# Attention and decay masks: added by VectorE instead of by TensorE

## The chip, the cores and the metric

One core of a Trainium2 chip runs the whole program. The metric is the device time of one execution in microseconds (us), taken as the median of several runs. The engines are TensorE (PE, matrix products; PEld is its weight load), VectorE (DVE), ScalarE (ACT), GpSimd (POOL) and SyncE (SP, which issues the DMAs here).

## The reference

The reference is a decoder trunk of two layers over 256 tokens with a model width of 1024, in float32. Each layer is a feed-forward half step, a mixing step, a second feed-forward half step and an input embedding. The mixing step projects the normalised tokens once and feeds two mixers from it: a gated recurrent one in matrix form (four heads of 256, causal, with learned decay) and an attention with a window of 128 tokens (16 query heads of 64, 4 key heads, a learned sink for each head). Cut to what matters here:

```python
scores = einsum(q, k) * 64 ** -0.5
scores = where(valid, scores, -inf)            # a causal band of 128
mx = maximum(max(scores, -1), sink)
pr = exp(scores - mx)
den = sum(pr, -1) + exp(sink - mx)
out = einsum(pr / den, v)

dlog = where(causal, b_t - b_s + i_s, -inf)    # the recurrent mixer's decays
w_intra = exp(dlog - m_t)
s = einsum(q, k) * w_intra
```

## The kernel before

The kernel keeps its tokens as two tiles of 128 rows (`NT` = 2). Every product with a weight is made of three: weights and activations are split into a high part (`wh`, written by ScalarE) and a low part (`wl`, written by VectorE from the raw weight minus the high part), and TensorE adds up high x high, high x low and low x high in PSUM. A weight unit of 128x1024 is called a part; a ring of eight parts (`RING`) lies between the splitting and TensorE. Raw weights of 1 MB come in by DMA, two parts each.

The four engines' queues are written out by hand, in the order in which the program's Python code runs. A planner, `Clock`, keeps a modelled time for each engine: it charges each product its output columns at 2400 to the microsecond and each VectorE instruction 0.12 us and its columns at 960 to the microsecond (`COST`, line 65; `charge`, line 92). Work beside the main products runs in chains: Python generators that give out some instructions and then yield. `tick` (line 196) is called between products and advances each chain whose modelled inputs are ready. So what TensorE finds next in its queue is fixed before the run, by modelled times. TensorE takes its queue in that order, and so do VectorE and ScalarE.

A layer's jobs are, in order: the first feed-forward block (65 parts), then in the mixing step the projection to keys, values and queries (`kvq`, 12 parts), the recurrent values (`v`, 8), a gate (`gt`, 8), recurrent queries and keys (`z`, 8), the attention's output product (`ya`, 8), the output gate (`og`), `z`, `gt`, `ym`, `yo`, and after these the second feed-forward block and the embedding.

The attention's chains lie beside `kvq`, `v` and `gt`. `groups` (called from `mix`) starts one `scores` chain for each pair of key heads p and each token tile t, four a layer. `scores` handles two key heads (g = 0, 1), each with four query heads, and takes S = 128 keys at t = 0 (four heads to a PSUM bank, one round) and S = 256 keys at t = 1 (two heads to a bank, two rounds). Six such rounds, called blocks here, make up a layer. In a block TensorE first adds the mask into each bank with one product of 512 columns (the identity in bf16 times the band, `sc<-band,identb`), then adds the score products, which use 64 rows of the array each (`sc<-kT,qT`). VectorE takes the maxima of all heads of a bank in one reduction (`mx<-sc`) and combines them with the sinks (`mx<-mx,nsink`). ScalarE takes the exponentials from PSUM into an SBUF slot (`pr<-sc,mx`) with the row's sum as a second output. The `outputs` chain (line 1220) divides (`pr<-pr,dn`), transposes on TensorE (`tp<-ident,pr`), splits the result (`ptd`) and multiplies by the values (`ha`).

`decays` (line 1017), beside `z` and `ya`, makes for each of four recurrent heads a bank of 384 columns: one product that spreads the decay rows (`wt<-rows,pick`), two masks of 128 columns on TensorE (`wt<-mask_st,identb`), and three exponentials by ScalarE (`w<-wt,gcols`). The `head` chain uses them later: its products are `st`, and VectorE multiplies by the decays (`ws<-st,w`).

PSUM has eight banks, handed out in rotation to all of these.

Of the kernel before, what the change touches and what calls it, by code (L numbers as in the profile page):

```python
# [13 lines left out]
BF16 = mybir.dt.bfloat16  # L14
AF = mybir.ActivationFunctionType
ALU = mybir.AluOpType
AX = mybir.AxisListType
PSUM = bass.MemoryType.PSUM

P = 128  # L20
# [12 lines left out]
NEG = -1e30  # L33
# [130 lines left out]
class Trunk:  # L164
# [84 lines left out]
    def consts(self):  # L249
        nc, c = self.tc.nc, self.const  # L250
        self.ident = c.tile([P, P], F32, name="ident")
        make_identity(nc, self.ident)
        self.identb = c.tile([P, P], BF16, name="identb")
        nc.vector.tensor_copy(self.identb, self.ident)
        self.mhalf = c.tile([P, 32], F32, name="mhalf")
        nc.vector.memset(self.mhalf, -0.5)
        self.h = [c.tile([P, D], F32, name=f"h{t}") for t in range(NT)]
        self.ones = c.tile([MH, P], F32, name="ones")
        nc.vector.memset(self.ones, 1.0)
        self.pick = c.tile([P, MH], F32R, name="pick")  # L260
        self.rows2 = c.tile([P, T + P], F32R, name="rows2")
        for x in (self.pick, self.rows2):
            nc.gpsimd.memset(x.bitcast(F32), 0.0)
        for r in (slice(0, MH), slice(32, 32 + MH)):
            nc.vector.tensor_copy(self.pick[r], self.ident[r, r])

        def mask(out, base, step, channel):

            nc.gpsimd.memset(out, 0.0)
            nc.gpsimd.affine_select(out=out, in_=out, compare_op=ALU.is_ge, fill=NEG, base=base,  # L270
                                    pattern=[[step, P]], channel_multiplier=channel)

        self.mask_st = c.tile([P, P], BF16, name="mask_st")
        mask(self.mask_st, 0, 1, -1)
        self.band = c.tile([P, 2 * P], BF16, name="band")
        mask(self.band[:, :P], -1, 1, -1)
        mask(self.band[:, P:], 0, -1, 1)
# [607 lines left out]
class Mlstm:  # L885
# [131 lines left out]
    def decays(self):  # L1017

        tr, nc = self.tr, self.nc
        N = T + P  # L1020
        for hd in range(MH):
            ps = tr.bank("wt")[:, :N]
            nc.tensor.matmul(ps, tr.pick[:, hd : hd + 1].to_broadcast([P, P]), tr.rows2, start=True, stop=False,
                             skip_group_check=True)
            for o in (slice(0, P), slice(T, N)):
                nc.tensor.matmul(ps[:, o], tr.identb, tr.mask_st, start=False, stop=True, skip_group_check=True)
            yield
            if hd % 2 == 0:
                two = tr.slot("w")[:, : 2 * N].rearrange("p (h t) -> p h t", h=2)
            w = two[:, hd % 2, :]  # L1030
            for i in range(3):
                o = slice(i * P, (i + 1) * P)
                nc.scalar.activation(w[:, o], ps[:, o], AF.Exp, bias=self.cols[:, i, hd : hd + 1])
            self.w.append(w)
            yield
# [61 lines left out]
class Swa:  # L1097
# [85 lines left out]
    def scores(self, t, p, acc, chains):  # L1183


        tr, nc = self.tr, self.nc
        S = (t + 1) * P
        per = NB // S
        tok = slice(t * P, (t + 1) * P)
        rows = [slice(g * AD, (g + 1) * AD) for g in range(2)]  # L1190
        hd = [slice(4 * (2 * p + g), 4 * (2 * p + g) + 4) for g in range(2)]
        pr = [tr.slot("pr")[:, : 4 * S].rearrange("p (j s) -> p j s", j=4) for _ in range(2)]
        mx, den = ([tr.col(n, 4) for _ in range(2)] for n in ("mx", "dn"))
        mask = tr.band[:, None, 2 * P - S :].to_broadcast([P, per, S])
        for j0 in range(0, 4, per):
            js = slice(j0, j0 + per)
            ps = [tr.bank("sc").rearrange("p (j s) -> p j s", j=per) for _ in range(2)]
            for g in range(2):
                nc.tensor.matmul(ps[g], tr.identb, mask, start=True, stop=False, skip_group_check=True)
            for j in range(per):  # L1200
                for x, y in ((0, 0), (0, 1), (1, 0)):
                    for g in range(2):
                        nc.tensor.matmul(ps[g][:, j, :], self.qT[x](4 * p + j0 + j, tok, p=rows[g]),
                                         self.kT[rows[g], y, p, :S], start=False, stop=x == 1, skip_group_check=True)
            yield
            for g in range(2):
                nc.vector.tensor_reduce(mx[g][:, js], ps[g], axis=AX.X, op=ALU.max)
                nc.vector.scalar_tensor_tensor(mx[g][:, js], mx[g][:, js], -0.125, self.nsink[:, hd[g]][:, js],
                                               op0=ALU.mult, op1=ALU.min)
            yield  # L1210
            for g in range(2):
                for j in range(per):
                    i = j0 + j
                    nc.scalar.activation(pr[g][:, i, :], ps[g][:, j, :], AF.Exp, scale=0.125, bias=mx[g][:, i : i + 1],
                                         accum_out=den[g][:, i : i + 1])
        for g in range(2):
            chains.append(tr.later(self.outputs(t, p, g, acc, hd[g], pr[g], mx[g], den[g])))
            self.haT.written(chains[-1], 4 * p, 4, t)
# [63 lines left out]
```

## Time and profile before

| | |
|---|---|
| median of three runs | 1383.12 us (1381.99 to 1383.64) |
| profiled execution | 1383.27 us |
| its span, first to last instruction | 1381.5 us |
| TensorE busy | 1366.2 us (99%) |
| VectorE busy | 860.7 us (62%) |
| ScalarE busy | 734.8 us (53%) |
| mean granted TensorE clock | 0.998 |

The profile is that of one execution. Its busy times are sums of drawn durations. On TensorE products are pipelined and their ends are modelled, so successive ones overlap in the drawing, and the distance between two starts tells what a product takes of the queue. An engine that is not the bound can be idle at no cost. In the rows an idle time in brackets names what ended it.

### The profile page before, as it was taken

How to read it: one execution, taken by the hardware profiler on the slowest of the kernel's cores; microseconds unless marked ns; L12 is line 12 of the kernel's file. 1: busy time of each engine (PE TensorE's matmuls, PEld its weight loads, DVE VectorE, ACT ScalarE, POOL GpSimd, SP SyncE). 2: the span in 40 equal slices, each digit the busy share in tenths (PEclk: the TensorE clock that was granted, in tenths of full speed). 3: DMA queues.
4: the chain of work that ended last, by engine and by line, in shares of the span. 5: the costliest groups of instructions: out<-in, count | busy, mean ns of one | idle time of the engine just before them, and what ended most of it. 6: DMA issues, size and time to landing. Idle time of an engine off the chain costs nothing.

```text
span 1381.5 us, 21941 instructions
## 1 busy us (share of the span) xinstructions
PE 1366.2 (99%) x9056; PEld 1233.3 (89%) x9056; DVE 860.7 (62%) x1213; ACT 734.8 (53%) x1146; POOL 55.4 (4%) x84
## 2 busy tenths in 40 slices
PE   8999999999999999999999999999999999999998
PEld 5999887899899899988879998878998998999886
DVE  5655458767786665554565554687677876554544
ACT  5554346878465444443454443477785554544433
POOL 0000012000000000000000000120000000000000
PEclk9999999999999999999999999999999999999999
DMA  6665636344645565565456566445456544755651
GB/s 206 222 212 168 229 125 212 123 138 110 226 153 185 167 213 186 169 232 184 158 162 213 170 199 213 152 154 173 106 143 206 181 156 164 220 190 187 209 180 61
DMA packets 125830, 243.81 MB, mean 176 GB/s; under 512 B 14977, under 2 KB 23841, under 8 KB 125730
## 3 DMA queue, kind: packets, MB, share of 16 engines
q1 hardware_dynamic: 125730, 242.41, 55.1%
q8 instruction: 71, 1.16, 0.4%
q14 instruction: 29, 0.24, 0.1%
HBM read 241.34 MB, written 1.05 MB: 175 GB/s over the span
## 4 chain that ended last, share of the span: by engine, by line
PE 96%; DMA 1%; DVE 1%; ACT 1%; issue 0%; POOL 0%; SPq 0%; ACTq 0%; POOLq 0%
PE dn L130 17%; PE pg L130 16%; PE pu L130 14%; PE gu L130 7%; PE z L130 7%; PE gt L130 7%; PE kvq L130 5%; PE ya L130 3%; PE v L130 3%; PE ym L130 3%; PE yo L130 3%; PE og L130 3%; PE tp L130 3%; PE sc L130 1%; PE ha L130 1%; DMA raw<-in_ffn_w_gate_dram 1%
## 5 line engine op out<-in xcount | busy, mean ns | idle before, releaser
L130 DVE TENSOR_TENSOR wl<-raw,wh 128x1024 fp32r<-128x1024 f32 (+1 forms) x448 | 540.2, 1222 | 351.3 <-ACT wh L130 348.5
L130 ACT CAST wh<-raw 128x1024 fp32r<-128x1024 f32 x448 | 460.5, 1050 | 414.1 <-PE dn L130 82.9
L130 PE MATMUL dn<-wh,hid 128*128 128x512 f32 x688 | 218.1, 395 | 0.0
L130 PE MATMUL pg<-uT,wh 128*128 128x256 f32 x1088 | 194.0, 281 | 0.0
L130 PE MATMUL pu<-uT,wh 128*128 128x256 f32 x1088 | 192.9, 280 | 0.0
L130 PEld LDWEIGHTS pg<-uT,wh 128*128 128x128 f32 x1088 | 166.4, 188 | 0.2
L130 PEld LDWEIGHTS pu<-uT,wh 128*128 128x128 f32 x1088 | 166.2, 188 | 0.0
L130 PEld LDWEIGHTS dn<-wh,hid 128*128 128x128 f32 x688 | 129.2, 188 | 30.2
L130 PE MATMUL pg<-uT,wl 128*128 128x256 f32 x544 | 152.4, 280 | 0.0
L130 PE MATMUL pu<-uT,wl 128*128 128x256 f32 x544 | 152.2, 280 | 0.0
L130 PE MATMUL dn<-wl,hid 128*128 128x512 f32 x352 | 139.0, 395 | 0.0
L130 PEld LDWEIGHTS pu<-uT,wl 128*128 128x128 f32 x544 | 102.4, 188 | 0.0
L130 PEld LDWEIGHTS pg<-uT,wl 128*128 128x128 f32 x544 | 102.3, 188 | 0.0
L130 PE MATMUL z<-uT,wh 128*128 128x256 f32 x512 | 93.5, 284 | 0.0
L130 PE MATMUL gt<-uT,wh 128*128 128x256 f32 x512 | 93.1, 283 | 0.0
L130 PE MATMUL gu<-wh,uT 128*128 128x512 f32 x256 | 83.4, 402 | 2.2 <-ACT uT L130 2.2
L130 PEld LDWEIGHTS gt<-uT,wh 128*128 128x128 f32 x512 | 78.8, 188 | 1.2
L130 PEld LDWEIGHTS dn<-wl,hid 128*128 128x128 f32 x352 | 66.1, 188 | 15.1
L130 PEld LDWEIGHTS z<-uT,wh 128*128 128x128 f32 x512 | 78.8, 188 | 0.6
L130 PE MATMUL z<-uT,wl 128*128 128x256 f32 x256 | 71.9, 281 | 0.0
L130 PE MATMUL gt<-uT,wl 128*128 128x256 f32 x256 | 71.8, 280 | 0.0
L130 PE MATMUL kvq<-wh,uT 128*128 128x512 f32 x192 | 63.7, 401 | 0.0
(194 smaller groups left out, 2037.7 us busy)
## 6 DMA issues: line engine op xcount, KB each, us to landing
raw<-in_w_in_dram SPq DMA_DIRECT2D x60, 1024.0 KB, 5.1
raw<-in_ffn_w_up_dram SPq DMA_DIRECT2D x40, 1024.0 KB, 5.1
raw<-in_ffn_w_down_dram SPq DMA_DIRECT2D x40, 1024.0 KB, 5.2
raw<-in_ffn_w_gate_dram SPq DMA_DIRECT2D x39, 1024.0 KB, 5.5
raw<-in_w_branch_a_dram SPq DMA_DIRECT2D x16, 512.0 KB, 5.9
raw<-in_w_branch_m_dram SPq DMA_DIRECT2D x8, 1024.0 KB, 5.1
raw<-in_w_out_dram SPq DMA_DIRECT2D x8, 1024.0 KB, 5.2
raw<-in_ple_gate_w_dram SPq DMA_DIRECT2D x8, 1024.0 KB, 8.0
```

The costliest lines, as they stand in the source:

```text
L130: return issue(*args, **kw)
```

## The change

The bf16 copy of the identity goes. In `decays` the two mask products go; after the row product the chain yields, then VectorE adds the mask to the two blocks of 128 columns in place in PSUM, the chain yields again, and ScalarE takes the exponentials as before. In `scores` the mask product of each bank goes, and the first score product of a bank starts the bank. For each query head VectorE runs one instruction that adds the mask to the head's scores, writes the sum to the SBUF slot `pr` and gives the row's maximum as a second output; it takes the place of the one reduction over all heads of the bank. ScalarE then takes the exponentials from `pr` into `pr`.

```diff
@@ -250,8 +250,6 @@
         nc, c = self.tc.nc, self.const
         self.ident = c.tile([P, P], F32, name="ident")
         make_identity(nc, self.ident)
-        self.identb = c.tile([P, P], BF16, name="identb")
-        nc.vector.tensor_copy(self.identb, self.ident)
         self.mhalf = c.tile([P, 32], F32, name="mhalf")
         nc.vector.memset(self.mhalf, -0.5)
         self.h = [c.tile([P, D], F32, name=f"h{t}") for t in range(NT)]
@@ -1020,14 +1018,14 @@
         N = T + P
         for hd in range(MH):
             ps = tr.bank("wt")[:, :N]
-            nc.tensor.matmul(ps, tr.pick[:, hd : hd + 1].to_broadcast([P, P]), tr.rows2, start=True, stop=False,
-                             skip_group_check=True)
+            nc.tensor.matmul(ps, tr.pick[:, hd : hd + 1].to_broadcast([P, P]), tr.rows2, start=True, stop=True)
+            yield
             for o in (slice(0, P), slice(T, N)):
-                nc.tensor.matmul(ps[:, o], tr.identb, tr.mask_st, start=False, stop=True, skip_group_check=True)
-            yield
+                nc.vector.tensor_tensor(ps[:, o], ps[:, o], tr.mask_st, op=ALU.add)
             if hd % 2 == 0:
                 two = tr.slot("w")[:, : 2 * N].rearrange("p (h t) -> p h t", h=2)
             w = two[:, hd % 2, :]
+            yield
             for i in range(3):
                 o = slice(i * P, (i + 1) * P)
                 nc.scalar.activation(w[:, o], ps[:, o], AF.Exp, bias=self.cols[:, i, hd : hd + 1])
@@ -1191,27 +1189,29 @@
         hd = [slice(4 * (2 * p + g), 4 * (2 * p + g) + 4) for g in range(2)]
         pr = [tr.slot("pr")[:, : 4 * S].rearrange("p (j s) -> p j s", j=4) for _ in range(2)]
         mx, den = ([tr.col(n, 4) for _ in range(2)] for n in ("mx", "dn"))
-        mask = tr.band[:, None, 2 * P - S :].to_broadcast([P, per, S])
+        mask = tr.band[:, 2 * P - S :]
         for j0 in range(0, 4, per):
             js = slice(j0, j0 + per)
             ps = [tr.bank("sc").rearrange("p (j s) -> p j s", j=per) for _ in range(2)]
-            for g in range(2):
-                nc.tensor.matmul(ps[g], tr.identb, mask, start=True, stop=False, skip_group_check=True)
             for j in range(per):
                 for x, y in ((0, 0), (0, 1), (1, 0)):
                     for g in range(2):
                         nc.tensor.matmul(ps[g][:, j, :], self.qT[x](4 * p + j0 + j, tok, p=rows[g]),
-                                         self.kT[rows[g], y, p, :S], start=False, stop=x == 1, skip_group_check=True)
+                                         self.kT[rows[g], y, p, :S], start=j + x + y == 0, stop=x == 1,
+                                         skip_group_check=True)
             yield
             for g in range(2):
-                nc.vector.tensor_reduce(mx[g][:, js], ps[g], axis=AX.X, op=ALU.max)
+                for j in range(per):
+                    i = j0 + j
+                    nc.vector.tensor_tensor_reduce(pr[g][:, i, :], ps[g][:, j, :], mask, 1.0, NEG, op0=ALU.add,
+                                                   op1=ALU.max, accum_out=mx[g][:, i : i + 1])
                 nc.vector.scalar_tensor_tensor(mx[g][:, js], mx[g][:, js], -0.125, self.nsink[:, hd[g]][:, js],
                                                op0=ALU.mult, op1=ALU.min)
             yield
             for g in range(2):
                 for j in range(per):
                     i = j0 + j
-                    nc.scalar.activation(pr[g][:, i, :], ps[g][:, j, :], AF.Exp, scale=0.125, bias=mx[g][:, i : i + 1],
+                    nc.scalar.activation(pr[g][:, i, :], pr[g][:, i, :], AF.Exp, scale=0.125, bias=mx[g][:, i : i + 1],
                                          accum_out=den[g][:, i : i + 1])
         for g in range(2):
             chains.append(tr.later(self.outputs(t, p, g, acc, hd[g], pr[g], mx[g], den[g])))
```

## Rows read from the trace of the kernel before

**Rows 1.** The page: one line of part 1 (busy us, share of the span, count, by engine) and the first line of part 4 (shares of the chain that ended last).
```profile
PE 1366.2 (99%) x9056; PEld 1233.3 (89%) x9056; DVE 860.7 (62%) x1213; ACT 734.8 (53%) x1146; POOL 55.4 (4%) x84
...
PE 96%; DMA 1%; DVE 1%; ACT 1%; issue 0%; POOL 0%; SPq 0%; ACTq 0%; POOLq 0%
```

**Rows 2.** Busy time by stretch: stretch, its us, busy us and count of PE, PEld, DVE, ACT and POOL, granted clock, DMA share, GB/s. The attention of layer 0 and the end of layer 0.
```profile
238.00:268.00 30.00, 30.00 (x172) 23.81 (x169) 22.60 (x49) 25.90 (x74) 2.87 (x10) 1.00 0.36 108
268.00:301.00 33.00, 32.54 (x260) 30.26 (x259) 19.81 (x38) 26.33 (x71) 0.00 (x0) 1.00 0.41 137
...
656.00:700.00 44.00, 41.02 (x183) 33.26 (x182) 26.06 (x35) 22.68 (x39) 2.56 (x3) 0.96 0.41 131
```

**Rows 3.** The waits of TensorE over the whole span: who waited for whom, us in total, times, longest.
```profile
PE tp L130 <- DVE xn L130: 3.9, 2, 3.0
...
PE sc L130 <- DVE ptd L130: 0.9, 2, 0.5
```

**Rows 4.** The instructions on the tiles `sc` and `wt`: durations in ns (least, median, most), first and last start, forms with counts.
```profile
L130 PEld LDWEIGHTS sc<-kT,qT x192: 182/186/189, 234.5 to 970.5; 64*128 64x128 f32 x192
...
L130 PE MATMUL sc<-band,identb x24: 376/384/390, 233.9 to 969.7; 128*128 128x512 bf16 x24
...
L130 PE MATMUL wt<-mask_st,identb x16: 219/224/230, 322.8 to 1020.9; 128*128 128x128 bf16 x16
```

**Rows 5.** TensorE's products in order of time around the first score block: start, us drawn, engine, line, operation, tiles, count.
```profile
233.69 0.39 PE L130 MATMUL kvq<-wh,uT 128*128 128x512 f32 x1
233.92 0.61 PE L130 MATMUL sc<-band,identb 128*128 128x512 bf16 x2
234.46 1.56 PE L130 MATMUL sc<-kT,qT 64*128 64x128 f32 x24
```

**Rows 6.** The same around the last score block of layer 0.
```profile
284.96 0.39 PE L130 MATMUL sc<-band,identb 128*128 128x512 bf16 x1
285.82 0.38 PE L130 MATMUL sc<-band,identb 128*128 128x512 bf16 x1 [0.46 <-DVE ptd L130]
286.12 0.98 PE L130 MATMUL sc<-kT,qT 64*128 64x256 f32 x12
```

**Rows 7.** The same around the first decay head of layer 0.
```profile
322.64 0.34 PE L130 MATMUL wt<-rows,pick 128*128 128x384 f32 x1
322.82 0.29 PE L130 MATMUL wt<-mask_st,identb 128*128 128x128 bf16 x2
322.92 0.48 PE L130 MATMUL z<-uT,wh 128*128 128x256 f32 x2
```

**Rows 8.** Groups of instructions of the whole span by shape: count, busy us, mean ns of one, idle time before them.
```profile
L130 DVE TENSOR_TENSOR wl<-raw,wh 128x1024 fp32r<-128x1024 f32 x444 | 535.4, 1222 | 344.9 <-ACT wh L130 342.1 <-PE pg L130 1.9
...
L130 ACT ACTIVATE pr<-sc,mx 128x256 f32<-128x256 f32 x32 | 14.8, 492 | 0.0
...
L130 ACT ACTIVATE pr<-pr,dn 128x256 f32<-128x256 f32 x32 | 13.3, 505 | 0.0
...
L130 DVE TENSOR_REDUCE mx<-sc 128x2 f32<-128x512 f32 x16 | 11.0, 686 | 5.6 <-PE sc L130 5.4
...
L130 DVE SCALAR_TENSOR_TENSOR og<-num,rd,og 128x256 f32<-128x256 f32 x16 | 7.7, 484 | 0.6
...
L130 DVE TENSOR_TENSOR vpad<-kvq,vpad 128x128 fp32r<-128x128 f32 x8 | 2.3, 286 | 0.7 <-ACT vpad L130 0.7
...
L130 DVE TENSOR_TENSOR_SCAN gates<-ones,gates 4x128 f32<-4x128 f32 x6 | 2.3, 403 | 0.1
...
L130 DVE TENSOR_TENSOR sg<-sg,pu 128x256 f32<-128x256 f32 x4 | 1.7, 422 | 4.8 <-PE pu L130 4.8
```

**Rows 9.** VectorE in order of time behind the first score blocks.
```profile
237.57 0.17 DVE L130 SCALAR_TENSOR_TENSOR mx<-mx,nsink 128x4 f32<-128x4 f32 x1
...
239.51 0.16 DVE L130 SCALAR_TENSOR_TENSOR mx<-mx,nsink 128x2 f32<-128x2 f32 x1
```

**Rows 10.** VectorE's weight subtractions (tile `wl`) from the start of the span to two moments: stretch, its us, busy us and count, granted clock, DMA share, GB/s.
```profile
0.00:238.50 238.50, 100.01 (x84) 1.00 0.61 199
...
0.00:346.20 346.20, 130.41 (x109) 1.00 0.56 175
```

**Rows 11.** ScalarE in order of time behind the same blocks: the first exponential of the second group of the first block, and the first of the second block.
```profile
240.24 0.38 ACT L130 ACTIVATE pr<-sc,mx 128x128 f32<-128x128 f32 x1
...
241.61 0.52 ACT L130 ACTIVATE pr<-sc,mx 128x256 f32<-128x256 f32 x1
```

**Rows 12.** ScalarE's divisions of the first block, and TensorE's transposes of them, in order of time.
```profile
252.04 1.27 ACT L130 ACTIVATE pr<-pr,dn 128x128 f32<-128x128 f32 x4
...
253.87 0.60 PE L130 MATMUL tp<-ident,pr 128*128 128x128 f32 x4
```

**Rows 13.** VectorE and ScalarE in order of time beside the last decay head of layer 0.
```profile
332.52 5.79 DVE L130 SCALAR_TENSOR_TENSOR cv<-z,feat,cv 128x255 f32<-128x255 f32 x12 [0.23 <-ACT cv L130]
...
338.83 2.36 DVE L130 TENSOR_TENSOR wl<-raw,wh 128x1024 fp32r<-128x1024 f32 x2
...
337.88 0.90 ACT L130 ACTIVATE w<-wt,gcols 128x128 f32<-128x128 f32 x3
```

**Rows 14.** TensorE in order of time at the first recurrent head of layer 0.
```profile
348.86 1.49 PE L130 MATMUL st<-qk,qk 128*128 128x256 f32 x12
```

## The prediction

> **What bounds the kernel now.** I read the busy shares first. TensorE is busy 1366.2 us, 99% of the span, VectorE 62%, ScalarE 53%, and 96% of the chain of work that ended last is TensorE [rows 1]. So the time is the sum of what TensorE issues, and the other two engines matter only where they make it wait. The stretches say where that happens. In the attention part of layer 0, 238 to 301 us, TensorE is busy 62.5 of 63 us at the full granted clock (1.00, that is 2.4 GHz); 3 us are idle at the layer's end, 656 to 700 [rows 2]. In the list of TensorE's waits these have names: 3.9 us for normalised rows, which nothing here touches, and 0.9 us, in two waits, for a PSUM bank in the attention [rows 3]. What is taken from TensorE's queue in these stretches should therefore come off the time nearly whole, if the chains beside it still finish in time.
>
> **What is removed from TensorE.** The 24 mask products of the scores (384 ns each as drawn) and the 16 of the decays [rows 4]. Drawn durations overlap; what counts is the distance between starts. Before a score block, full-width products start every 0.23 us: the last at 233.69, the two masks from 233.92, and the first score product at 234.46 [rows 5]. The pair thus takes 0.54 us, of which 2 x 0.23 = 0.46 is the products and 0.08 the change to half-height tiles. Without the masks that change follows an ordinary product. If it then costs nothing the pair was worth 0.54; if the scores' weight load (0.186 us, [rows 4]) now stands open instead, 0.54 - 0.19 = 0.35. I take 0.46, since the change of tiles stays and masks and products have the same size. Twelve pairs (24 masks): 12 x 0.46 = 5.5 us, bounds 4.2 and 6.5.
>
> At one block in each layer the gain is smaller. At 284.96 the first mask starts, the second waits until 285.82 for a bank that VectorE frees (the subtraction for `ptd`), and the scores start at 286.12 [rows 6]. Without masks the scores wait for the same bank and can start at 285.82: 0.30 in place of 0.46, for two layers -0.3 us. The scores' own banks come free earlier than now (VectorE is their last reader, no longer ScalarE), but that is not the bank waited for here, so I count nothing for it.
>
> In the decays the row product starts at 322.64, the two masks at 322.82 and the next weight product at 322.92 [rows 7]: 0.10 us for a pair. Eight pairs: 0.8 us, or nothing if the next product's weight load, hidden behind the masks now, stands open. The cast copy of the identity at the start goes too; it lies under the first loads and is worth nothing.
>
> Sum on TensorE: 5.5 - 0.3 + 0.8 = 6.0 us.
>
> A page differs a little. The Trainium skill, "TensorE: Matmul & The Clock Gate", section "Wait — 56ns, not 53.3ns?", gives 2.4 GHz columns plus some 2.5 ns for each product, 215.7 ns at 512 columns and 55.6 ns at 128. By it the 40 masks were worth 24 x 0.2157 + 16 x 0.0556 = 6.1 us where the rows give 5.5 + 0.8 = 6.3 us; the rows' 0.23 us is the larger, and the sum keeps it.
>
> **What is added to VectorE.** A score block is two groups of four (128 keys) or two of two (256 keys) heads. Today each group is one reduction of 128x512, 686 ns [rows 8], and a small minimum, which stays. Then there are 32 sum-and-maximum instructions of 128x128 and 32 of 128x256, in place of 24 reductions. The trace has no such instruction. From below: a plain two-input operation, 286 ns at 128 columns and 422 at 256 [rows 8]. From above: the scan, which carries a value along the row as the maximum does, 403 ns at 128 columns [rows 8]; going by its excess over the plain one (0.117 us at 128, twice that at 256) some 656 at 256. I take the three-input operation, 484 ns at 256 [rows 8], and with the step of 136 ns between the plain ones some 350 at 128, because three operations on one element are nearest to it. VectorE's work: 32 x 0.35 + 32 x 0.484 = 26.7 us for 24 x 0.686 = 16.5; with the decay adds, 16 x 0.286 = 4.6, it grows by 14.8 us, 7.4 a layer. That is not on TensorE's path as long as two covers hold.
>
> First cover: the split weights. Behind the longer block on VectorE stand weight subtractions (1222 ns each, [rows 8]). By 238.5 us 84 of them have begun [rows 10]; the first feed-forward block uses 65 parts and the projection to queries, keys and values 12, so 7 are ahead when the values start there. A part lasts 12 products of 0.23 us, 2.8 us: a lead of some 19 us against some 1 us of delay a block. If this cover were gone, each block would cost its overrun, 0.6 to 1.4 us.
>
> Second cover: ScalarE's exponentials start late anyway. A block of 128-key heads grows from 1.37 to 8 x 0.35 = 2.8 us, so its last minimum, now at 237.57 to 237.74, moves to 239.2; the second group's first exponential is at 240.24, behind those of the first group [rows 9, 11]. Slack 2.5 us against 1.43 (upper price 1.85). A block of 256-key heads grows by 4 x 0.484 - 1.37 = 0.56 us (upper price 1.25); its first minimum ends at 239.67 and the exponentials on it start at 241.61 [rows 9, 11], slack 1.9. So the exponentials should start within some 0.5 us of where they do. Then come the divisions and TensorE's transposes, which have 0.56 us of slack at the nearest place: the last division of the group ends at 253.31 and its transpose starts at 253.87 [rows 12].
>
> **What moves.** The exponentials read SBUF instead of PSUM. The row for the same shape from SBUF (`pr<-pr,dn`, 128x256) is 505 ns, from PSUM 492 [rows 8]: 13 ns more, 64 times, 0.8 us of ScalarE and none of it on the path. A page speaks more strongly against this move: the Trainium skill, "VectorE: DVE Perf Modes", section "The TRN2 errata — SBUF-src ops pay a fixed extra latency per instruction", has 224 cycles fixed for ScalarE from SBUF and 172 from PSUM, at 1.2 GHz 43 ns each, by which ScalarE would lose 64 x 0.043 = 2.8 us. This trace shows a third of it, and either way it is lost within ScalarE's slack. The `pr` slot is now first written by VectorE, some 2.5 us earlier; if the slot is not yet free, VectorE waits and the weight subtractions behind it, under the first cover. In the decays the adds go into VectorE's queue between the row product and the exponentials, behind convolution runs of up to 5.79 us (332.52, [rows 13]); ScalarE then holds weight casts behind its exponentials. The last decay exponential is at 337.88 [rows 13] and the first head's product, which the code gives out only once that head's decay rows are asked for, at 348.86 [rows 14]: 10 us of cover. The lead in weights is thinnest here: 109 subtractions begun by 346.2 [rows 10] when 106 parts are used up, 3 parts.
>
> **Rivals.** (a) The transposes become the wait. The kernel's own planner places them in TensorE's queue by its clock, and charges a mask pair 2 x 512/2400 = 0.43 us, so the places should move by nearly what is saved. If they stay, TensorE reaches 253.87 three pairs, 1.4 us, early and waits 0.8 there; as much again behind the other three pairs, whose slack I take as no greater: 1.6 us a layer, 1377.1 + 3.2 = 1380.3. For it: ScalarE is busy 25.9 of 30 us there [rows 2]. (b) The weight store runs dry at 346. The 107th part, first used just after 346.2, is written by the first of the two subtractions that begin at 338.83, so by 340.05 [rows 13]: 6.2 us ahead. If a whole convolution run (5.79 us) and the two subtractions behind it (2.36, [rows 13]) come between an add and its exponentials, ScalarE holds the casts behind them 8.2 us, and TensorE waits 2.0 us a layer: 1377.1 + 4.0 = 1381.1, no change that can be measured. Against it: the planner charges the added work to its clock and gives the exponentials out later instead. (c) Slower: the new instruction is far dearer than any row. The second cover ends where 8 instructions of 128 exceed 1.37 + 2.5 + 0.56 us, at 0.55 us each. At 1.2 us (a weight subtraction, [rows 8]) the first block is 8 x 1.2 - 1.37 = 8.2 us late, 5.2 beyond its slack of 3.06, and a layer has two such blocks: 1377.1 + 10.4 = 1387.5 if one of them is felt, 1397.9 if both, and I take 1392. Against: it streams the same 128 columns as rows of 0.29 to 0.40 us; for: no row shows what a sum with a running maximum and an extra output costs to set up.
>
> **How the numbers follow.** The profiled execution took 1383.27 us, 1.8 more than its span, and the median is 1383.12. From the median, 1383.1 - 6.0 = 1377.1 us. The forecast's own range is 1375.8 (12 x 0.54 + 0.8) to 1379.2 (12 x 0.35 - 0.3, nothing from the decays). Chances: forecast 0.60, below it 0.04, (a) 0.14, (b) 0.10, (c) 0.12. A measurement here can tell about 0.2%, 2.8 us, so faster means below 1380.3, which takes half of (a): 0.60 + 0.04 + 0.07 = 0.71; same 0.07 + 0.10 = 0.17; slower 0.12. Leaving out (c), the part below and the dearer end of (b), 0.04, gives 0.80 in 1375.8 to 1383.
>
> **What would show it.** Right: TensorE's busy time about 6 us less, starts at a score block going from an ordinary product to scores within 0.3 us, TensorE's waits unchanged but for the bank, VectorE up by 12 to 20 us, new instructions of 0.3 to 0.65 us. Wrong: new waits of the transposes for `pr` (a), of `ya` products for `wl` near 346 (b), or sum-and-maximum rows above 0.55 us (c).

## The result and the profile after

The kernel after takes 1374.53 us (median of 4 runs, 1373.99 to 1375.79), the kernel before in the same job 1382.55 us (4 runs, 1381.21 to 1383.64): ratio on record 0.9950, 95% interval 0.9938 to 0.9962. Over the later jobs the kernel before stands between 1381.5 and 1381.7 us, and the kernel after, run again, at 1374.54. So the change is worth some 7.2 us (1381.7 - 1374.5; by the means of all runs on record 6.9), where 6.0 were forecast; one such interval is some 3 us wide, so it is the traces below that must tell 7.2 from 6.0. The sign was right; the time lies 1.3 us below the range and 2.6 us below the forecast, 1.4 of it because the forecast started from 1383.1, a median of three runs (1383.1 - 1381.7), and 1.2 because the change is worth more. The profiled execution took 1374.73 us, with a span of 1372.9.

The page of the kernel after: busy us, share of the span and count by engine, then the chain that ended last.

```profile
PE 1359.6 (99%) x9016; PEld 1231.6 (90%) x9016; DVE 867.7 (63%) x1332; ACT 738.7 (54%) x1148; POOL 58.3 (4%) x84
...
PE 91%; DMA 3%; DVE 3%; ACT 1%; issue 0%; POOL 0%; SPq 0%; ACTq 0%; POOLq 0%
```

TensorE has 40 products fewer and is busy 6.6 us less than in [rows 1]; VectorE is busy 7.0 us more, not the 12 to 20 that the forecast named. TensorE's waits in the kernel after, all that the view lists (us in total, times, longest):

```profile
PE tp L130 <- DVE xn L130: 3.5, 2, 2.1
PE g L130 <- DMA row<-in_ffn_norm_dram: 2.3, 1, 2.3
PE gu L130 <- ACT uT L130: 1.5, 1, 1.5
PE gu L130 <- DVE wl L130: 0.8, 1, 0.8
```

Against [rows 3] one line is gone: `sc` no longer waits for `ptd`. The forecast had kept that wait. Now TensorE in order of time around the first score block, the last one of layer 0, and the first decay head:

```profile
233.49 0.39 PE L130 MATMUL kvq<-wh,uT 128*128 128x512 f32 x1
233.81 1.84 PE L130 MATMUL sc<-kT,qT 64*128 64x128 f32 x24
...
286.93 0.28 PE L130 MATMUL gt<-uT,wl 128*128 128x256 f32 x1
287.14 0.98 PE L130 MATMUL sc<-kT,qT 64*128 64x256 f32 x12
288.05 0.50 PE L130 MATMUL gt<-uT,wh 128*128 128x256 f32 x2
...
327.01 0.28 PE L130 MATMUL z<-uT,wl 128*128 128x256 f32 x1
327.13 0.34 PE L130 MATMUL wt<-rows,pick 128*128 128x384 f32 x1
327.30 0.40 PE L130 MATMUL ya<-qT,wh 128*128 128x256 f32 x2
```

From the last ordinary product to the first score product it is 0.32 us (233.49 to 233.81) where [rows 5] has 0.77 (233.69 to 234.46): a pair of masks was worth 0.45 us. At the last block the scores start 0.21 us behind the product ahead of them, without a wait; in [rows 6] the first mask alone stands 1.16 us ahead of them. From the row product of a decay head to the next weight product it is 0.17 us, against 0.28 in [rows 7].

What VectorE and ScalarE do instead, by shape: count, busy us, mean ns of one, idle time before.

```profile
L130 ACT ACTIVATE pr<-pr,mx 128x256 f32<-128x256 f32 x32 | 15.9, 501 | 0.0
...
L130 ACT ACTIVATE pr<-pr,mx 128x128 f32<-128x128 f32 x32 | 12.4, 390 | 0.2
L130 DVE CUSTOM_DVE_ANT_0 pr<-sc,band 128x256 f32<-128x256 f32 x32 | 12.2, 419 | 0.9 <-PE sc L130 0.8
...
L130 DVE CUSTOM_DVE_ANT_0 pr<-sc,band 128x128 f32<-128x128 f32 x32 | 7.4, 286 | 0.6 <-PE sc L130 0.6
...
L130 DVE DVE_READ_ACCUMULATOR2_ANT mx<- 128x1 f32 x64 | 5.3, 83 | 0.0
L130 DVE TENSOR_TENSOR wt<-wt,mask_st 128x128 f32<-128x128 f32 x16 | 4.8, 297 | 0.7 <-PE wt L130 0.4
```

And VectorE in order of time behind the first score block:

```profile
235.68 0.29 DVE L130 CUSTOM_DVE_ANT_0 pr<-sc,band 128x128 f32<-128x128 f32 x1
235.90 0.08 DVE L130 DVE_READ_ACCUMULATOR2_ANT mx<- 128x1 f32 x1
235.90 0.28 DVE L130 CUSTOM_DVE_ANT_0 pr<-sc,band 128x128 f32<-128x128 f32 x1
...
237.69 0.17 DVE L130 SCALAR_TENSOR_TENSOR mx<-mx,nsink 128x4 f32<-128x4 f32 x1
237.77 1.22 DVE L130 TENSOR_TENSOR wl<-raw,wh 128x1024 fp32r<-128x1024 f32 x1
```

The sum-and-maximum is drawn as long as a plain two-input operation (286 and 419 ns; [rows 8] has 286 and 422), and its second output comes from an extra instruction of 83 ns drawn beside the next one. The step from one head to the next is 0.22 us (235.68 to 235.90), below the forecast's lower bound of 0.286. Eight heads with both minima end at 237.86, 2.2 us after they start.

### The profile page after: what moved, and what is told of

Same layout as the page of the kernel before. It is cut to its first block, busy times and chain, and to the rows that moved or that the text cites. A ratio compares the mean times of both kernels' runs of the same rounds, so it can differ in the third digit from the quotient of the medians.

```text
span 1372.9 us, 21950 instructions
## 1 busy us (share of the span) xinstructions
PE 1359.6 (99%) x9016; PEld 1231.6 (90%) x9016; DVE 867.7 (63%) x1332; ACT 738.7 (54%) x1148; POOL 58.3 (4%) x84
## 3 DMA queue, kind: packets, MB, share of 16 engines
q8 instruction: 71, 1.16, 0.3%
## 4 chain that ended last, share of the span: by engine, by line
PE 91%; DMA 3%; DVE 3%; ACT 1%; issue 0%; POOL 0%; SPq 0%; ACTq 0%; POOLq 0%
PE dn L130 17%; PE pg L130 16%; PE pu L130 14%; PE gt L130 7%; PE z L130 7%; PE gu L130 6%; PE v L130 3%; PE ya L130 3%; PE ym L130 3%; PE og L130 3%; PE yo L130 3%; PE kvq L130 3%; PE tp L130 2%; DVE wl L130 1%; DMA raw<-in_ffn_w_gate_dram 1%; DMA raw<-in_w_in_dram 1%
```

## The experiments

Two theories of the 1.2 us by which the change is worth more. Theory 1: the two bank waits are gone, with the masks as forecast. Theory 2: it is the end of layer 0, where the execution profiled of the kernel before had products at half speed behind its wait for `xn` (a granted clock of 0.96 in the stretch 656 to 700 of [rows 2]) and the one of the kernel after had not. And two theories of why the bank waits went. Theory A: VectorE's larger charge in the planner moved the places in TensorE's queue. Theory B: the scores' banks come free earlier, since VectorE and no longer ScalarE reads them last.

**The two kernels again**, no edit.

> The kernel before, unchanged, once more: a second profile of it and the noise of the comparison. If the wait of 2.98 us at the end of layer 0 and the half-speed products behind it (1.2 GHz, 693.9 to 697.6 us) belong to its order of instructions, they stand here again; if they were an accident of the one execution, the wait is nearer the 2.08 us of the changed kernel and the products behind it run at 2.4 GHz. Ratio 1.000 within 0.002. The two waits for a PSUM bank at the last score block of each layer, 0.46 us, should stand again either way.

> The changed kernel once more, in the same job. Theory 1 (masks 12 x 0.45, decays 8 x 0.10, the two bank waits gone, 2 x 0.62, in sum 7.4 us): 1375.2 of 1382.6, ratio 0.9946. Theory 2 (the order at the end of layer 0 is better too, 1.4 us more): 1373.8, ratio 0.9936. Theory 3 (the forecast's 6.0 us, the rest is noise): 1376.6, ratio 0.9957.

Measured: 1381.51 us (ratio to the kernel before 0.9997, 0.9989 to 1.0006) and 1374.54 us (0.9948, 0.9935 to 0.9960). In the new execution of the kernel before, TensorE waits for `xn` 3.0 us in all and no products run at half speed behind it (granted clock 1.00), and the ratio of the kernels is the same (0.9948 and 0.9950). Theory 2 falls by that trace; the interval of e2 by itself holds the ratios of all its three theories. The bank wait stands as it did. TensorE in order of time around the last score block, in the kernel before run again:

```profile
283.71 0.60 PE L130 MATMUL tp<-ident,pr 128*128 128x128 f32 x4
...
284.73 0.28 PE L130 MATMUL gt<-uT,wl 128*128 128x256 f32 x1
284.85 0.39 PE L130 MATMUL sc<-band,identb 128*128 128x512 bf16 x1
285.71 0.38 PE L130 MATMUL sc<-band,identb 128*128 128x512 bf16 x1 [0.46 <-DVE ptd L130]
286.01 0.50 PE L130 MATMUL sc<-kT,qT 64*128 64x256 f32 x4
```

And on VectorE the subtraction for which the second mask waits:

```profile
284.96 0.69 DVE L130 TENSOR_TENSOR ptd<-tp,ptd 128x512 fp32r<-128x512 f32 x1 [0.46 <-ACT ptd L130]
```

From 284.73 to 286.01 it is 1.28 us, and 0.21 in the kernel after. The last block of a layer thus gained 1.07 us, 0.62 beyond the 0.45 of the masks; two layers, 1.24 us.

**Each part alone.** e3 is the kernel after with the decays of the kernel before (masks there by TensorE); e4 is the kernel before with the decays of the kernel after.

> The attention's masks by VectorE as in the changed kernel, the decays' masks by TensorE as before. Theory 1: the score blocks carry 12 x 0.45 + 2 x 0.62 = 6.6 us, 1376.0, ratio 0.9952, and no wait for a bank. Theory 3 (as forecast, bank waits stay and take part of the gain): 5.2 us, 1377.4, ratio 0.9962, and waits of PE for a bank at the last score block.

> The decays' masks by VectorE as in the changed kernel, the attention as before. All theories: 8 x 0.10 = 0.8 us less, 1381.8, ratio 0.9994, with both bank waits still there; a rival in which VectorE's adds hold up ScalarE and the weights behind it: 0 to 2 us more, with waits of ya products for wl near 346 us.

Measured: e3 1376.05 us (0.9960, 0.9948 to 0.9973), e4 1381.92 us (1.0003, 0.9994 to 1.0012). e3 has no bank wait, e4 has both. The attention's part carries most of it, 5.7 of 7.2 us. In e4 the eight decay heads count 0.10 us less each, as forecast, but a transposition in the second feed-forward block of layer 1 waits, the products behind it run slower (the block's `pg` products take 95.45 us, 93.66 in the kernel before run again), and nothing is left. The new line among TensorE's waits in e4, beside the old one:

```profile
PE sc L130 <- DVE ptd L130: 0.9, 2, 0.5
PE tp L130 <- DVE sg L130: 0.6, 1, 0.6
```

**The masks put back as products of zeros**, in the kernel after:

```diff
+            for g in range(2):
+                nc.tensor.matmul(ps[g], tr.zeros, mask[:, None, :].to_broadcast([P, per, S]), start=True, stop=False, ...)
```

> The changed kernel with one more product of 512 columns on TensorE in front of each score bank, whose stationary side is zero, so that it adds nothing: the mask's price on TensorE alone, with the whole of VectorE's new work in place. By the counts of starts 12 x 0.45 = 5.4 us more than the changed kernel: 1379.9 of 1381.7, ratio 0.9987; if the bank waits come back with these products, 1.2 us more, ratio 0.9996. If VectorE's work had cost TensorE something that the removed products hide, the kernel would be slower than the one before: above 1.000.

Measured: 1380.06 us (0.9990, 0.9981 to 0.9999), 5.5 us over the kernel after, without a bank wait. TensorE around the first score block of e6:

```profile
233.36 0.39 PE L130 MATMUL kvq<-wh,uT 128*128 128x512 f32 x1
233.59 0.61 PE L130 MATMUL sc<-band,zeros 128*128 128x512 bf16 x2
234.13 1.56 PE L130 MATMUL sc<-kT,qT 64*128 64x128 f32 x24
```

Again 0.77 us (233.36 to 234.13). The masks' term of the forecast, 12 x 0.46 = 5.5 us, is shown.

**Banks held longer, in the kernel after; places moved, in the kernel before.** e5 writes the masked scores back into PSUM, where ScalarE reads them, so that the banks are held as before. e7 is the kernel before with `tr.clock.charge("vector", 230 if t == 0 else 0)` after each maximum, which adds 0.36 us for a group of 128-key heads and 0.12 for one of 256-key heads, so that the planner gives each block the VectorE time that it gives it in the kernel after.

> The changed kernel, but VectorE writes the masked scores back into PSUM and ScalarE reads them there, so that a score bank is held until the exponentials are done, as before the change; the planner's charges and so the order on TensorE stay those of the changed kernel. Theory A (the bank waits went because the planner's places moved): no wait of PE for a bank, 1374.6 of 1381.7, ratio 0.9948. Theory B (they went because VectorE frees the score banks earlier): the waits are back at the last score block of each layer, 0.5 us or more each, ratio 0.9956 or above. ScalarE's exponentials take 383 and 492 ns again in place of 390 and 501, with no effect on the time.

> The kernel before, with one thing changed: after each maximum the planner is told that VectorE takes longer (0.36 us for four heads, 0.12 for two, as its charges for the new instructions do), so that the places of the attention's later steps in TensorE's queue move; no instruction is added. Theory A: both bank waits go and with them 2 x 0.62 = 1.2 us: 1380.5 of 1381.7, ratio 0.9991. Theory B: they stay, ratio 1.000.

Measured: e5 1375.51 us (0.9958, 0.9944 to 0.9972), e7 1382.39 us (1.0007, 0.9998 to 1.0016). Neither has a bank wait. Places moved are thus enough to end it, and e5 alone looked like the end of theory B. But e7 gained nothing: its score blocks count 1.24 us less, as they should, and as much came back at other places.

**The planner's books turned back**, in the kernel after. e10 charges VectorE what the old reduction cost (512 columns a group). e11 keeps the decays' masks on TensorE and charges the attention's two masks too, though they are gone, so that every product left stands in the order of the kernel before (the code is cut to the lines that matter):

```diff
+            for g in range(2):
+                tr.clock.charge("tensor", NB)
...
-                    nc.vector.tensor_tensor_reduce(...)
+                    tr.tc.nc.vector.tensor_tensor_reduce(...)      # e10 too
+                tr.clock.charge("vector", NB)                      # e10 too
```

> The kernel after, with its sum-and-maximum instructions off the planner's books and one charge of 512 columns (0.65 us) for each group, which is what the old reduction was charged. So the masks are gone from TensorE and from its planned time, and VectorE's planned time is that of before. The order on TensorE comes out different from both kernels'. Theory A (the bank waits went because VectorE's larger charge moved the places in TensorE's queue): the wait of `sc` for `ptd` comes back at the last block of each layer, some 0.5 us each, and the score blocks count 16.9 + 1.2 = 18.1 us; the time is 1375.5 to 1376.5. Theory A' (the masks leaving TensorE's planned time is enough to move the places): no bank wait, blocks 16.5 to 17, and the time is that of the kernel after within its other order, 1373.5 to 1376.

> Only the attention part of the change, with the planner's books as before: the sums and maxima uncharged, one charge of 512 columns of VectorE for each group and two of 512 columns of TensorE for each block in place of the masks that are gone. Every product left then stands in TensorE's queue exactly in the order of before (the decays keep their masks there). This is the forecast's own case, in which nothing but the masks goes. Forecast's term for the bank: `sc` still waits for `ptd` at the last block of each layer, longer by what TensorE comes early, the block counting (from the product ahead of it to the one behind) some 1.28 - 0.16 = 1.1 us in place of 1.28, the score blocks 23.2 - 10 x 0.45 - 2 x 0.16 = 18.4 us, and the time 1376 to 1377. Theory B (earlier freeing of the score banks takes the wait away): no bank wait, 16.6 us, 1374.5 to 1375.5. The forecast's case (a), places that stay: new waits of the transposes for `pr`, 1.6 us a layer, 1379 to 1380.5.

Measured: e10 1376.58 us (0.9965, 0.9953 to 0.9977), e11 1376.09 us (0.9961, 0.9948 to 0.9975), both without a bank wait. For the attention e11 is the forecast's own case, nothing but the masks gone from TensorE's queue, and the wait is gone with the old places. Theory A is not needed; theory B ends the wait by itself. The time of e11 alone would speak the other way: it lies where the forecast's term was expected (1376 to 1377), above theory B's 1374.5 to 1375.5; e10 lies above both its ranges. The trace decides, and where the rest was lost stands under what stays open. TensorE in order of time around the last block of layer 0 in e11:

```profile
281.42 0.60 PE L130 MATMUL tp<-ident,pr 128*128 128x128 f32 x4
...
282.45 0.28 PE L130 MATMUL gt<-uT,wl 128*128 128x256 f32 x1
282.66 0.98 PE L130 MATMUL sc<-kT,qT 64*128 64x256 f32 x12
```

And VectorE's subtraction for the transposes of 281.42:

```profile
282.68 0.69 DVE L130 TENSOR_TENSOR ptd<-tp,ptd 128x512 fp32r<-128x512 f32 x1 [0.47 <-ACT ptd L130]
```

The scores start before that subtraction does, so they don't stand in its bank. The compiled programs list each tile's bank. For the two `sc` tiles of the last block, who held their banks last, the same in both layers:

```
kernel              first sc tile, bank of       second sc tile, bank of
before, e4          tp (first transposes)        tp (second transposes)
e11, e10            sc (block before, group 1)   ha (long free)
after, e3, e6,
e8, e9              sc (block before, group 0)   sc (block before, group 1)
e5, e7              tp (first transposes)        sc (block before, group 0)
```

So the eight banks are not handed out in a fixed rotation, as the section on the kernel has it: e11 asks for its tiles at this place in the order of the kernel before and gets other banks. In the kernel before, ScalarE's exponentials are the last to read the banks of the block before, only just ahead of the last block in the program, and the last block gets the transposes' banks. With VectorE as the last reader the block before is done with earlier in the program, and the last block takes one or two of its banks. In e5 and e7 ScalarE reads last again, but the last block stands later, and one of the banks is free by then. By which rule the allocator chooses among free banks, no run here was made to show.

**The new instruction dearer.** In the kernel after each sum-and-maximum is given out twice (e8) and four times (e9) with the same result, the extra ones uncharged.

> The changed kernel with each sum-and-maximum given out twice, the first of each pair unknown to the planner: 18 us more of VectorE in all. A block of 128-key heads grows by 1.7 us, one of 256-key heads by 1.4. If the second cover holds as forecast (3.06 us of slack for a 128-key block, of which the change uses 0.5), the time stays: 1374.6, ratio 0.9948. If the slack is used up already, 12 blocks x up to 1.5 us come back: 1375 to 1392, with new waits of the transposes.

> The kernel after, with each sum-and-maximum four times (the same result; three of the four uncharged). A head of 128 keys then takes 0.84 us of VectorE and one of 256 keys 1.4, a price between the forecast's end of the cover (0.55) and its dear case (1.2). Twice the instruction cost 4.75 us with TensorE waiting for transposes of `qn`. The forecast's own case (c) by its formula: 8 x 0.84 - 1.37 = 5.35 us late, 2.3 beyond the slack of 3.06, at two blocks a layer: 9 us over the kernel after, 1383.7, with waits of the transposes of `pr`. What e8 showed (work queued behind the instruction on VectorE is late, beyond a cover of some 6.6 us of 9 a layer, then one for one): 27 - 6.6 = 20 us a layer if every instruction lies ahead of the same waiter, 1415; in proportion to what was added, 3 x 4.75 = 14.3 us, 1389, with waits for `qn` first and for `pr` or `ptd` besides.

Measured: e8 1379.29 us (0.9989, 0.9981 to 0.9998), 4.8 over the kernel after; e9 1431.84 us (1.0366, 1.0347 to 1.0385), 57 over. Every expectation for e9 was too low. The waits of TensorE that are new in e8, then those of e9:

```profile
PE tp L130 <- DVE qn L130: 3.3, 4, 1.2
```

```profile
PE tp L130 <- DVE qn L130: 16.3, 2, 8.3
PE sc L130 <- DVE mx L130: 8.0, 4, 2.5
PE ha L130 <- DVE mx L130: 6.6, 2, 3.6
...
PE tp L130 <- ACT pr L130: 2.8, 2, 1.6
...
PE ha L130 <- DVE ptd L130: 2.1, 3, 0.8
```

First it is the transposes of the normalised queries `qn`: VectorE's products for them are queued behind the sums, as VectorE in e8 shows (the sum of the last head, the minimum, then `qn`). The second pair waits besides for GpSimd's factor `r`, whose input VectorE makes in the same queue:

```profile
244.80 0.42 DVE L130 CUSTOM_DVE_ANT_0 pr<-sc,band 128x256 f32<-128x256 f32 x1
245.15 0.08 DVE L130 DVE_READ_ACCUMULATOR2_ANT mx<- 128x1 f32 x1
245.27 0.16 DVE L130 SCALAR_TENSOR_TENSOR mx<-mx,nsink 128x2 f32<-128x2 f32 x1
...
246.14 0.75 DVE L130 TENSOR_TENSOR qn<-kvq,r 128x256 f32<-128x256 f32 x2
```

In e9 the waits shown sum to 35.8 us. TensorE is also busy 21.1 us longer than in the kernel after, with the same products (its mean granted clock is 0.982, 1.000 in the kernel after), and 35.8 + 21.1 = 56.9, all of the 57. TensorE behind the longest wait, and the stretch around it (its us, busy us and count of PE, PEld, DVE, ACT, POOL, granted clock, DMA share, GB/s):

```profile
255.74 1.11 PE L130 MATMUL tp<-ident,qn 128*128 128x128 f32 x4 [8.30 <-DVE qn L130]
256.50 0.78 PE L130 MATMUL v<-wh,uT 128*128 128x512 f32 x1
257.08 0.63 PE L130 MATMUL v<-wl,uT 128*128 128x512 f32 x1
257.50 0.63 PE L130 MATMUL v<-wh,uT 128*128 128x512 f32 x1
257.93 1.05 PE L130 MATMUL tp<-ident,qn 128*128 128x128 f32 x4
```

```profile
230.00:260.00 30.00, 20.13 (x116) 15.67 (x115) 26.30 (x122) 14.67 (x37) 3.54 (x10) 0.80 0.18 61
```

After 8.3 us idle the products from 257.08 on start 0.42 to 0.43 us apart, not 0.23: the lower of the two clocks, 1.2 GHz (granted clock 0.50 from 256 to 258 us). In e9 as a whole the waits are paid with their own length and more than half as much again.

## Why the prediction was right or wrong

**What bounds the kernel, and the masks' price: right.** TensorE's queue sets the time, and a pair of masks costs 0.45 us of it (forecast 0.46): the starts around the first block show it in the kernel after, and e6 takes 5.5 us back. The page of the Trainium skill that the prediction set against it, "TensorE: Matmul & The Clock Gate", section "Wait — 56ns, not 53.3ns?", has 0.2157 us for a product of 512 columns; e6 gives 5.5 / 24 = 0.23, the rows' price, though the intervals of the two times are too wide to exclude the page's.

**The step that failed: "for two layers -0.3 us", the bank at the last block.** The prediction said of the scores' own banks that they come free earlier, "but that is not the bank waited for here, so I count nothing for it". That holds only if each tile gets its bank in a fixed rotation, which the section on the kernel and the forecast took for granted. The banks go by what is free, and a bank set free earlier was taken by the last block. e11 shows it with the old order of products: no wait, and 1.07 us gained at each last block where the forecast had 0.30. In place of -0.3 stands 2 x 0.62 = +1.24 us. With it the count is 12 x 0.45 + 1.24 + 0.8 = 7.4 us; 7.2 were measured (in part by luck, see below). The term missed by 1.5 us; the forecast's lower end had the dearest mask pair and no gain from a bank, and with a start that was 1.4 us too high besides the time fell out of the range. In the change as made the places move as well, which ends the wait too (e7); either is enough.

**The decays: right in place, loose in the total.** 0.10 us a head at the place where they stood, in the kernel after and in e4. But e4 as a whole gained nothing and e3 is 1.5 us behind the kernel after. The total of such a small term isn't its count.

**VectorE's price: right in effect, too dear.** Taken were 0.35 and 0.484 us a head; the steps are 0.22 and 0.35 (from 239.25 to 239.60 in the kernel after), and VectorE grew by 7.0 us, not 14.8. Both covers held: no wait for `pr`, for `wl` near 346 or for the exponentials. In case (c) the price was far too high and the place was wrong: at twice the measured price (0.42 us for 128 columns, where the forecast saw cover up to 0.55) TensorE already waits, for `qn`, a part of VectorE's queue behind the sums that the prediction didn't list. At four times it is 57 us, where case (c) by its own formula had 9: the formula had neither `qn` nor the bank waits for the sums nor the clock.

**The other rivals.** Case (a), the places stay and the transposes wait for `pr`: e11 keeps the places exactly and has no such wait. Case (b): the projection's `ya` products wait for no `wl`.

**Exponentials from SBUF: the row was right.** 501 against 492 ns and 390 against 383 for 128 columns before, 7 to 9 ns more (13 forecast); e5, from PSUM again, has 493 and 371, so at most 19. By the figures of the page of the Trainium skill cited for it, "VectorE: DVE Perf Modes", section "The TRN2 errata — SBUF-src ops pay a fixed extra latency per instruction", the estimate was 43; this trace doesn't agree.

**What stays open.** The masks and waits count 6.6 us in e11, and its time is 5.5 less; 7.4 and 7.2 in the kernel after. Over the two mixing steps alone, from the first `kvq` product to the last `yo` product, the count holds in e11: 276.56 and 277.34 us, where the kernel before run again has 279.85 and 280.65, so 6.6 less. Outside them e11 loses: set product by product against the kernel before run again, 1.0 us at the end of layer 0, where the wait for `xn` is followed by a granted clock of 0.86 in 690 to 700, and 0.8 in the second feed-forward block of layer 1. There the same products in the same order run 0.7% slower for some 90 us, with the clock granted at 1.00 in both. Why wasn't found. The kernel after, run again, is 8.8 us shorter over its mixing steps (275.81 and 275.91 us), 1.4 more than counted, and loses 1.5 us to slower products in the second feed-forward blocks of the two layers. That 7.4 counted and 7.2 measured lie so close is thus in part luck; where the 1.4 come from wasn't traced.

## What to carry to other kernels

Before a wait for a buffer is kept in a sum, ask how the buffer was chosen: where an allocator gives out what is free, an earlier last reader changes who waits for whom, even for tiles that it doesn't touch; the compiled program's list of banks tells it without a run. When work is added to an engine that isn't the bound, list everything queued behind it up to the next thing that the bound engine needs, not only what the change writes. And a term of 0.1 us at each place is shown by its starts, not by the total, which moves by 1 us when the order does.

## What the runs showed of the hardware

- The sum with a running maximum and a second output costs no more than a plain two-input operation: 286 ns drawn at 128 columns and 419 at 256; its extra read of 83 ns lies beside the next instruction.
- The change from 128-row to 64-row tiles costs TensorE 0.09 us: 0.32 us from an ordinary 512-column product to the first score product, where ordinary ones stand 0.23 apart. Behind a 256-column product it is 0.21, where these stand 0.12 apart.
- The same 256-column products, in the same order and at a granted clock of 1.00, run at several paces. In the second feed-forward block of layer 1 it is 93.66 us from the first `pg` product to the last in both executions of the kernel before, 94.44 in e11 and 94.56 in both executions of the kernel after; in layer 0 93.79, 93.79 and 94.37. The pace belongs to the program, then, and not to the execution. Stretches of 20 us in layer 1, columns as above: the kernel before run again, e11 and the kernel after.

```profile
1220.00:1240.00 20.00, 20.00 (x173) 20.00 (x172) 11.07 (x11) 8.88 (x11) 0.00 (x0) 1.00 0.54 170
```

```profile
1215.00:1235.00 20.00, 20.00 (x172) 20.00 (x171) 11.40 (x12) 8.75 (x10) 0.00 (x0) 1.00 0.54 164
```

```profile
1215.00:1235.00 20.00, 20.00 (x171) 20.00 (x171) 10.98 (x12) 8.98 (x10) 0.00 (x0) 1.00 0.59 189
```

One or two products in 173 are lost. In e11 the transposes just ahead (`tp<-ident,sg`) start 0.15 us later than in the kernel before, counted from the products ahead of them; the pace then stays until the block ends. No run shows the cause.
